# A Strassen down-projection for four more blocks of the middle group, and fewer modulation steps in an opening head

## The chip, the core and the metric

The kernel runs on one core of a Trainium2 chip. The core has five engines, each with its own instruction stream: TensorE (PE, with its weight loads in a row of its own, PEld), VectorE (DVE), ScalarE (ACT), GpSimd (POOL) and SyncE (SP), whose queue issues nearly all transfers of this kernel, in order. The metric is device time in microseconds: of the kernel before, the median of 3 runs is 2173.13 (2171.32 to 2175.94).

## What is computed

One layer of a hybrid streaming encoder over 2112 tokens (2048 of a prompt and 64 of a second sequence) of width 1024, in float32:

```python
mod = (c_act @ w_ada + b_ada)[:, None, :]
sh1, sc1, gt1, sh2, sc2, gt2 = jnp.split(mod, 6, -1)
h = rmsnorm(x, g1) * (1 + sc1) + sh1
proj = h @ w_in
...
hs, C, n, m = mlstm_seq(q, k * HEAD_DIM ** -0.5, v, ig, lf, C, n, m)
...
x = x + gt1 * (jnp.concatenate([pool_out, hs], -1) @ w_out)
h2 = rmsnorm(x, g2) * (1 + sc2) + sh2
up = h2 @ w_up
upp = jnp.concatenate([conv_buf, up], 1)
conv = b_conv + sum(w_conv[j] * upp[:, j:j + T] for j in range(3))
a, g = jnp.split(conv, 2, -1)
x = x + gt2 * ((silu(g) * a) @ w_down)
y = rmsnorm(x, g_final)
```

`w_up` is 1024 x 5632 (two halves, a and g, of 2816 = 22 blocks of 128) and `w_down` 2816 x 1024. The modulation has 6 parts of 1024, from `w_ada`.

## The kernel before

**Precision.** Each float32 operand of a large matrix product is split into a rounded high part and the rest, and three matmuls (the list PASSES) make one product. For a weight unit of 128x512, ScalarE copies the high part (line 411) and VectorE subtracts it from the whole (line 414). Units come in a fixed order, the list `stream`, through the SP queue, some loads ahead.

**Attention part**, about the first 800 us: four groups of 512 tokens (the last of 576). Each has a v projection, four heads, the pooling mixer and an output projection. For a head, `proj_qko` makes q, k and the output gate by `gemm` (line 478), and `lstm` the recurrence; there kw (made on VectorE, helper line 250) feeds the matmuls of line 1323. Beside them run generators that give one step at a tick: lists `bg[0]` to `bg[4]`. `bg[3]` is the modulation: `ada` makes one part of it in 16 steps, each with a load of 128x512 of `w_ada` (line 194, tile raw), three steps ahead, and two VectorE operations (lines 208 and 210). `bg[4]` is `up_sums`, which makes sums of quarters of `w_up` for Strassen's scheme: two loads (line 857), four VectorE adds of 128x256 (876 to 881), one store to `wsum` (867). `gemm` ticks `bg[3]` once inside its loop and once at its end:

```python
        for i in (1,) if calm else (1, 3):
            tick(i)
```

`calm` is a list which is filled ahead of group 0's first head and emptied behind that head's `proj_qko`. In groups 1 to 3 it stays empty. The order of instructions on each engine is fixed when the kernel is built; in the attention groups by a scheduler, in the FFN as written.

**FFN part**, from about 800 us: three groups of 704 tokens. In every group a class `Pair` handles one block f of a and g: its up-projection is Strassen's scheme, seven products of 12 matmuls of 352 columns (line 1594), whose partial results are combined by ScalarE and VectorE (lines 1603, 1607, 1641, 1724); then the convolution's three taps (the first on ScalarE, line 1567, two on VectorE, line 1572), silu (1781), the gate's product (1786, 1789) and the split of the result (`split_hi`, `split_lo`, 1864, 1869). All are put between the next pair's products.

Several blocks at a time are projected down and added to x. `PARTS` says which: group 0 has parts of 5, 5, 6, 6 blocks, groups 1 and 2 parts of 4, 4, 4, 4, 6. Parts of four blocks in groups 1 and 2 (`paired`) go by Strassen's scheme too: the quad is held until the next pair's products have been issued, and `quad_down` then makes it, 168 matmuls of 352 columns (line 2037) with 14 weight units (from `w_quad` and from `dsum`, sums that `quad_sums` makes in group 0), 24 additions to x (`rows_add`, line 2009), and copies of partial sums from one bank to another. One product of the current pair (`last_product`) and its combinations go between them. In place of a copy, ones times a tile can open a bank (`seed`, `take(True)`). The other parts go by `down` (line 2160): per row block n (8) and block k, three matmuls for each of two sections of 448 and 256 columns; block 20's gate and block 21's taps stand in `todo` and are taken one by one between them.

**Between two FFN groups.** `prepare` (in `bg[1]`) normalizes the next group's input and stores seven combinations of it (B11, T1, T2, B21, B22, T3, T4) in DRAM; `reload` loads them (line 692) in the last part of the group. In that last part, `fsq_acc` squares each finished row of x on ScalarE (line 2000) and adds it up on POOL (line 2001), and in the next group's first products `final` (in `bg[0]`) makes the last norm (lines 1901, 725, 726, 1910) and stores y (line 1914).

Of the kernel before, what the change touches and what calls it, by code (L numbers as in the profile page):

```python
# [9 lines left out]
F32 = mybir.dt.float32  # L10
F32R = mybir.dt.float32r
AF = mybir.ActivationFunctionType
ALU = mybir.AluOpType
# [18 lines left out]
ENDS = ((0, 448), (448, 704))  # L32
PARTS = (((0, 5), (5, 10), (10, 16), (16, 22)),) + (((0, 4), (4, 8), (8, 12), (12, 16), (16, 22)),) * 2
NQ = 4

# [29 lines left out]
def tile_layer(ctx: ExitStack, tc: tile.TileContext, xT, vecs, cst, rst, w_mod, w_ada, w_qkou, w_v, w_pool,  # L65
# [264 lines left out]

    dsum = dr.tile([8, P, 4, 512], F32, tag="dsum", name="dsum")

# [9 lines left out]
    for g in range(NFG):  # L342
        held = None
        late = []
        for (f0, f1_) in PARTS[g]:
            for f in range(f0, f1_):
                stream += [(up_unit(f, 0), 512), sum_unit(g, f, WS1)] + late
                stream += [sum_unit(g, f, WS2), (up_unit(f, 1), 512)] + [sum_unit(g, f, i) for i in (WS4, WS3)]
                late = [(up_unit(f, 3), 512)]
                if held is not None:  # L350
                    stream += quad_units(held, late)
                    held, late = None, []
            if paired(g, (f0, f1_)):
                held = f0 // NQ
                continue
            order = down_order(f1_ - f0)
            ends = g == NFG - 1 and f1_ == NF
            seen = set()
            for i, (n, k) in enumerate(order):
                if i == f1_ - f0 - 2:  # L360
                    stream += late
                c = f0 + k // 4 * 4
                if k % 4 == 0 or (n, c) not in seen:
                    seen.add((n, c))
                    d = min(c + 4, f1_)
                    stream.append((w_down[n, :, c * P:d * P], (d - c) * P, OUT, None, ends and n >= NE))
            late = []
# [477 lines left out]
    if True:  # L845
# [604 lines left out]
        for o in groups:  # L1450
# [28 lines left out]
            q1 = None  # L1479
            if o.g == 0:  # L1480
                calm.append(1)
            for hd in range(NH):
# [62 lines left out]
    def both_of(a, b):  # L1545
        return lambda: (a(), b())
# [34 lines left out]
    def behind():  # L1581

        while later:
            later.pop(0)()
# [33 lines left out]

    free = []

    def take(seeded=False):

        while len(free) + len(used) < 6:
            free.append(Bank())
        i = next((i for i, bk in enumerate(free) if bk.wide >= FH), 0) if seeded else 0
        bk = free.pop(i)
        used.append(bk)
        if seeded and bk.wide < FH:
            pe.matmul(bk.t[:, :FH], ones_r, B[-1].at("B11", 0, 0), start=True, stop=True)
            bk.start(FH)  # L1630
        return bk
# [11 lines left out]
    def quad_sums():  # L1643

        for d in range(8):
            for c in (0, 256):
                t = f2.tile([P, 2, FT], F32R, tag="av", name="qs", bufs=AVB)
                w = t.bitcast(F32).rearrange("p a t -> p (a t)")[:, :1024].rearrange("p (i c) -> p i c", i=4)
                nc.sync.dma_start(out=w, in_=w_quad[d, :, :, c:c + 256])
                for _ in range(5):  # L1650
                    yield
                a11, a12, a21, a22 = (w[:, i] for i in range(4))
                dve.tensor_tensor(out=a22, in0=a21, in1=a22, op=ALU.add)
                yield
# [32 lines left out]
    class Pair:  # L1687


        ended = False  # L1690
        quad = None

# [75 lines left out]
        def taps_a(self):  # L1768
            for j in (1, 0):
                conv_tap(self.o, self.f, self.ea, self.ta, j)  # L1770

        def last_product(self):
# [88 lines left out]
        def split_hi(self):  # L1861
            self.d = f2.tile([P, 2, FT], F32R, tag="av", name="av", bufs=AVB)
# [8 lines left out]

    def reload(Bo):
        for nm in BN:
            Bo.load(nm)
            yield
            yield
# [17 lines left out]

    def final(o, x3, ssum):
        for _ in range(4):
            yield
# [11 lines left out]
        for k in range(KD):  # L1909
            dve.scalar_tensor_tensor(out=x3[k], in0=x3[k], scalar=V[:, V_GF + k:V_GF + k + 1], in1=box[0],  # L1910
                                     op0=ALU.mult, op1=ALU.mult)
            yield
            yield
            nc.sync.dma_start(out=yT[k, :, o.t0:o.t0 + FT], in_=x3[k])
            yield
            yield

# [76 lines left out]

    def fsq_acc(ssum, src, lo, hi, first):
        if first:
            act.activation(ssum[:, lo:hi], src, AF.Square)
        else:
            s = fscr()
            act.activation(s[:, lo:hi], src, AF.Square)  # L2000
            pool.tensor_tensor(out=ssum[:, lo:hi], in0=ssum[:, lo:hi], in1=s[:, lo:hi], op=ALU.add)

# [8 lines left out]

    def quad_down(o, quad, cur, done):

# [6 lines left out]
        def duo(d):  # L2020
            units, banks = {}, {}

            def half_product(nm, role, X, op, first=False):
# [18 lines left out]
                if X == 1:  # L2042
                    live[0] -= 1
                behind()

# [32 lines left out]
            if d == 0:  # L2078
                cur.sum_g0()
                cur.shut = True  # L2080
            copy("2B", "1B")
            if d == 0:
# [28 lines left out]
    for o in fgroups:  # L2111
        Bo = B[o.g]
        held = None
        for pi, part in enumerate(PARTS[o.g]):
# [8 lines left out]
            for f in range(f0, f1_):  # L2123
                old, pair = pair, Pair(o, Bo, f, f - f0, av, quad)
                pair.products(old)
                if o.g == 0 and len(x3) < KD or pi == 0 and not bg[0]:
                    x3 += load_x2(o, range(len(x3), min(len(x3) + 2, KD)))
                if held is not None:
                    quad_down(o, held, pair, old)
                    held = None  # L2130
# [3 lines left out]
            if not o.last:  # L2134
# [4 lines left out]
                if lastp:  # L2139
                    drain(0, 1)  # L2140
                    B.append(Sums())
                    bg[1].append(reload(B[-1]))
            if lastp:
# [50 lines left out]

            old = pair.before
            todo.extend([both_of(pair.sum_g1, old.gate), both_of(pair.sum_a, old.split_hi), both_of(old.split_lo, pair.scale_a)])
            for n in range(NE - 1):
                bks.append([take() for _ in ENDS])
                down(bks[n], Ws[n], range(nf - 2), ENDS, plain=n == 0)
                if n == 0:  # L2200
                    do(9)
# [21 lines left out]
        if not o.last:  # L2223
            drain(1)
            bg[0].append(final(o, x3, ssum))
            x3 = []
# [87 lines left out]
```

## Time and profile before

| | |
|---|---|
| median of 3 runs | 2173.13 us |
| profiled execution | 2174.68 us |
| its span | 2172.9 us |
| granted TensorE clock | 0.998 |
| DMA, mean | 248 GB/s |
| attention part, FFN groups 0, 1, 2 begin near | 0, 800, 1258, 1710 us |

The profile is one execution. A row of a timeline has a start, a length, the engine, the line, the operation, what it writes and reads, its shape and, in brackets, how long the engine stood idle ahead of it and what ended that. A row with xN stands for N instructions. Lines that begin with a line number and an engine are groups: count, busy time, mean length in ns, idle time ahead of them.

### The profile page before, as it was taken

The numbers are of one execution on the slowest core, as the hardware profiler recorded it, in microseconds if no ns is written. First come the engines' busy times: TensorE is split into PE (matmuls) and PEld (weight loads), VectorE is DVE, ScalarE is ACT, GpSimd is POOL, SyncE is SP. The second block draws the span as 40 slices with busy tenths as digits, with TensorE's granted clock in tenths as the row PEclk, the third lists the DMA queues.
The fourth block names the chain that finished last, engine by engine and source line by source line (L and its number), as shares of the span: only waits on it lengthen the run. The fifth ranks groups of instructions, "written<-read, shape, count | busy, mean of one in ns | idle before, by whom it ended". The sixth has DMA issues, their size and how long they took to land.

```text
span 2172.9 us, 38060 instructions
## 1 busy us (share of the span) xinstructions
PE 2151.4 (99%) x13553; PEld 2044.4 (94%) x13553; DVE 1634.9 (75%) x3040; ACT 1096.1 (50%) x2181; POOL 258.4 (12%) x475
## 2 busy tenths in 40 slices
PE   8999999999999999999999999999999999999998
PEld 7888888888899999999999999999999999999998
DVE  5878668667955778797967668888886597887874
ACT  4554335334333446464736445655655365565554
POOL 0010000001000201010101220100101321111112
PEclk9999999999999999999999999999999999999999
DMA  8987997987888477888967976666668675555542
GB/s 319 328 305 233 323 321 246 309 302 244 301 283 288 169 260 239 282 292 300 350 214 255 321 245 222 234 208 209 228 222 274 223 255 186 170 177 190 171 160 77
DMA packets 297351, 539.51 MB, mean 248 GB/s; under 512 B 25760, under 2 KB 114336, under 8 KB 297160
## 3 DMA queue, kind: packets, MB, share of 16 engines
q1 hardware_dynamic: 286568, 511.87, 69.6%
q10 hardware_dynamic: 10592, 25.20, 3.0%
q8 instruction: 107, 1.75, 0.3%
q14 instruction: 84, 0.69, 0.1%
HBM read 410.98 MB, written 125.98 MB: 247 GB/s over the span
## 4 chain that ended last, share of the span: by engine, by line
PE 85%; DMA 5%; DVE 5%; issue 2%; ACT 2%; SPq 0%; POOL 0%; DVEq 0%; ACTq 0%; POOLq 0%
PE mm L1594 34%; PE mm L478 22%; PE mm L2160 12%; PE mm L2037 8%; PE mm L1133 3%; DVE wt L414 1%; DMA wt<-wsum 1%; PE m L1323 1%; DMA hl_kept<-wt 1%; PE m L1308 1%; PE m L1343 1%; PE m L1345 1%; DVE tg L1572 1%; DMA raw<-w_qkou 0%; ACT wt L411 0%
## 5 line engine op out<-in xcount | busy, mean ns | idle before, releaser
L1594 PE MATMUL mm<-hx,wt 128*128 128x352 f32 x5544 | 885.9, 321 | 0.7 <-DVE wt L414 0.5
L1594 PEld LDWEIGHTS mm<-hx,wt 128*128 128x128 f32 x5544 | 878.7, 188 | 2.6 <-DVE wt L414 2.0
L478 PE MATMUL mm<-hl,wt 128*128 128x512 f32 (+2 forms) x1920 | 387.4, 357 | 0.0
L411 ACT ACTIVATE wt<-raw 128x512 fp32r<-128x512 f32 (+3 forms) x470 | 276.6, 597 | 177.6 <-PE mm L478 52.8
L478 PEld LDWEIGHTS mm<-hl,wt 128*128 128x128 f32 x1920 | 316.4, 189 | 47.7 <-issue 4.4
L414 DVE TENSOR_TENSOR wt<-raw,wt 128x512 fp32r<-128x512 f32 (+3 forms) x470 | 312.8, 672 | 61.9 <-ACT wt L411 61.7
L2160 PE MATMUL mm<-av,wt 128*128 128x448 f32 (+1 forms) x1632 | 262.7, 322 | 0.0
L2160 PEld LDWEIGHTS mm<-av,wt 128*128 128x128 f32 x1632 | 250.4, 188 | 11.1
L2009 DVE SCALAR_TENSOR_TENSOR x<-mm,MOD,x 128x352 f32<-128x352 f32 (+3 forms) x360 | 167.5, 505 | 77.7 <-PE mm L2160 64.3
L2037 PE MATMUL mm<-av,wt 128*128 128x352 f32 x1344 | 220.7, 323 | 1.9 <-DVE x L2009 0.7
L2037 PEld LDWEIGHTS mm<-av,wt 128*128 128x128 f32 x1344 | 215.4, 188 | 5.0 <-DVE ea L1603 3.0
L1641 ACT ACTIVATE mm<-mm 128x352 f32<-128x352 f32 x196 | 87.8, 448 | 233.7 <-PE mm L1594 177.1
L478 PE MATMUL mm<-mx,wt 128*128 128x512 f32 (+1 forms) x960 | 182.9, 352 | 0.3 <-DVE scr L250 0.3
L478 PEld LDWEIGHTS mm<-mx,wt 128*128 128x128 f32 x960 | 159.4, 188 | 23.0 <-PE mm L478 0.5
L1572 DVE SCALAR_TENSOR_TENSOR ta<-ea,V,ta 128x704 f32<-128x704 f32 (+1 forms) x132 | 125.7, 953 | 58.4 <-ACT ta L1567 54.4
L1572 DVE SCALAR_TENSOR_TENSOR tg<-eg,V,tg 128x704 f32<-128x704 f32 (+1 forms) x132 | 125.7, 952 | 56.8 <-ACT tg L1567 54.3
L414 DVE TENSOR_TENSOR wt<-wt 128x512 fp32r<-128x512 f32 x196 | 133.0, 685 | 12.8 <-ACT wt L411 12.7
L411 ACT ACTIVATE wt<-wt 128x512 fp32r<-128x512 f32 x196 | 119.2, 622 | 36.6 <-DMA wt<-wsum 35.7
L1550 POOL COPY ea<-UC 128x2 f32<-128x2 f32 x66 | 33.1, 501 | 506.2 <-DVE ta L1572 407.3
L1781 ACT ACTIVATE tg<-tg 128x704 f32<-128x704 f32 (+1 forms) x66 | 52.5, 795 | 71.8 <-DVE tg L1572 71.8
L1133 PE MATMUL mm<-wt,hl 128*128 128x256 f32 (+1 forms) x576 | 71.4, 284 | 0.0
L1133 PEld LDWEIGHTS mm<-wt,hl 128*128 128x128 f32 x576 | 70.4, 190 | 0.8 <-issue 0.6
(305 smaller groups left out, 2207.0 us busy)
## 6 DMA issues: line engine op xcount, KB each, us to landing
wt<-wsplit SPq DMA_DIRECT2D x132, 512.0 KB, 4.3
raw<-w_up SPq DMA_DIRECT2D x198, 256.0 KB, 3.8
wt<-hl_kept SPq DMA_DIRECT2D x96, 512.0 KB, 6.3
wt<-wsum SPq DMA_DIRECT2D x132, 256.0 KB, 5.0
wsplit<-wt SPq DMA_DIRECT2D x66, 512.0 KB, 5.1
w<-w_up SPq DMA_DIRECT2D x88, 256.0 KB, 4.4
wsum<-w SPq DMA_DIRECT2D x44, 512.0 KB, 5.9
Bd<-fscr ACTq DMA_DIRECT2D x56, 352.0 KB, 4.3
```

Source lines behind the costliest of these rows:

```text
L411: act.activation(u.w[:, 0, :u.n], u.raw[:, :u.n], AF.Copy)
L414: dve.tensor_tensor(out=u.w[:, 1, :u.n], in0=u.raw[:, :u.n], in1=u.w[:, 0, :u.n].bitcast(F32), op=ALU.subtract)
L478: pe.matmul(ps[bi][:, :hi - lo], U[:, a, k % 4 * P:(k % 4 + 1) * P], mv[k][:, b, lo:hi], start=(at == 0 and pi == 0), stop=(k == order[-1] ...
L1133: pe.matmul(ps[ti][:n, :cols], h[4 * kh + k4][:, b, lo:lo + n], U[:, a, k4 % 2 * cols:(k4 % 2 + 1) * cols], start=(kh == 0 and k4 == 0 and ...
L1550: pool.tensor_copy(ext[:, 0:2], UC[:, f, :])
L1572: dve.scalar_tensor_tensor(out=t[:, :E], in0=ext[:, j:j + E], scalar=wc(j, f), in1=t[:, :E], op0=ALU.mult, op1=ALU.add)
L1594: pe.matmul(bk.t[:, :FH], U[:, a, kc * P:(kc + 1) * P], Bo.at(nm, kc, b), start=(first and kc == 0 and pi == 0), stop=(kc == 3 and pi == 2 ...
L1641: act.activation(to.t[:, :FH], bk.t[:, :FH], AF.Copy)
L1781: act.activation(self.tg[:, :E], self.tg[:, :E], AF.Silu)
L2009: dve.scalar_tensor_tensor(out=x3[n][:, a:b], in0=bk.t[:, a - lo:b - lo], scalar=gt2(n, s), in1=x3[n][:, a:b], op0=ALU.mult, op1=ALU.add)
L2037: pe.matmul(bk.t[:, :FH], U[:, a, c:c + P], quad.put(op, m, b), start=(first and m == 0 and pi == 0), stop=(m == 1 and pi == 2), skip_grou ...
L2160: pe.matmul(bks[i].t[:, :hi - lo], U[:, a, k % 4 * P:(k % 4 + 1) * P], av[k][:, b, lo:hi], start=(k == 0 and (a, b) == PASSES[0]), stop=(k ...
```

## The change

1. **Parts.** In the middle group (group 1) the last part of six blocks becomes a quad of blocks 16 to 19 and a plain part of blocks 20 and 21. `quad_sums` makes ten double sums in place of eight (16 more VectorE adds, 4 more loads and 4 more stores of 512 KB, in group 0).
2. **That quad** is held until the products of block 21 have been issued, and `quad_down` gets `last=True`: behind every second half product it takes one piece from `todo`: block 21's scale, its four taps one by one, silu, gate, split. Blocks 20 and 21 keep their results in tiles of the next group's inputs, so the last of these (T4) is loaded after the part; the other six are loaded in another order. A seed reads a tile of the quad (list `seeds`).
3. **Squares.** Group 1's rows are squared at the opening of the next group, in `final`, eight on ScalarE, with seven additions on VectorE in place of POOL's; its steps stand one or two ticks otherwise.
4. **Modulation.** `calm` is filled ahead of the first head of every attention group.

In the order of instructions, TensorE has 24 matmuls less (288 of line 2160 become 96 of it and 168 of line 2037), POOL 7 additions less, SP 14 quad units and 8 of 128x256 where there were 16 plain ones. In the attention part TensorE's order differs only in a few small matmuls of a modulation part that come one head later in group 3; VectorE's and SP's differ in groups 1 and 2.

```diff
-PARTS = (((0, 5), (5, 10), (10, 16), (16, 22)),) + (((0, 4), (4, 8), (8, 12), (12, 16), (16, 22)),) * 2
-NQ = 4
+PARTS = (((0, 5), (5, 10), (10, 16), (16, 22)), ((0, 4), (4, 8), (8, 12), (12, 16), (16, 20), (20, 22)),
+         ((0, 4), (4, 8), (8, 12), (12, 16), (16, 22)))
+NQ, QUADS = 4, 5
...
-                if held is not None:
+                if held is not None and (f1_ - f0 > 2 or f == f1_ - 1):
                     stream += quad_units(held, late)
...
-            if o.g == 0:
-                calm.append(1)
+            calm.append(1)
...
-            pe.matmul(bk.t[:, :FH], ones_r, B[-1].at("B11", 0, 0), start=True, stop=True)
+            pe.matmul(bk.t[:, :FH], ones_r, seeds[-1](), start=True, stop=True)
...
-        for d in range(8):
+        for d in range(2 * QUADS):
...
-    def reload(Bo):
-        for nm in BN:
+    def reload(Bo, names):
+        for nm in names:
...
-    def final(o, x3, ssum):
-        for _ in range(4):
+    def final(o, x3, ssum, squares):
+        for n in range(KD if squares else 0):
+            fsq_acc(ssum, x3[n], 0, FT, n == 0, dve)
+            yield
+        for _ in range(8 if squares else 4):
             yield
...
                 if X == 1:
                     live[0] -= 1
+                    if last:
+                        do()
...
+                if last:
+                    todo.extend([both_of(cur.scale_a, cur.scale_g)] + [cur.tap(*c) for c in ("a1", "a0", "g1", "g0")]
+                                + [cur.silu, cur.gate, cur.split_hi, cur.split_lo])
...
-                if held is not None:
+                if held is not None and nf > 2:
                     quad_down(o, held, pair, old)
...
+                    if nf == 2:
+                        for p in (old, pair):
+                            p.d = f1.tile([P, 2, HX], F32R, tag="hx", name="av", bufs=2 * len(BN))
                     B.append(Sums())
-                    bg[1].append(reload(B[-1]))
+                    bg[1].append(reload(B[-1], ("B11", "T1", "T2", "B21", "B22", "T3") if nf == 2 else BN))
+            if held is not None and nf == 2:
+                q = held
+                seeds.append(lambda: q.put("B11", 0, 0))
+                quad_down(o, q, pair, old, True)
+                behind()
+                do(9)
+                seeds.pop()
+                held = None
...
-                if not lastp:
+                if not lastp or nf == 2:
                     return
...
-            bg[0].append(final(o, x3, ssum))
+            if nf == 2:
+                Bn = B[-1]
+                Bn.load(BN[-1])
+            bg[0].append(final(o, x3, ssum, nf == 2))
```

More of the change, by code (lines that the diff above doesn't have):

```diff
@@ L329, in sum_unit @@
         return (kept, 512, WHOLE, None) if g else (wsum[f, :, i], 512, INSIDE, kept)
-    dsum = dr.tile([8, P, 4, 512], F32, tag="dsum", name="dsum")
+    dsum = dr.tile([2 * QUADS, P, 4, 512], F32, tag="dsum", name="dsum")
     def quad_units(p, first):
@@ L1619, in tile_layer @@
     free = []
+    seeds = [lambda: B[-1].at("B11", 0, 0)]
     def take(seeded=False):
@@ L1690, in tile_layer @@
         ended = False
-        quad = None
+        quad = d = None
         def __init__(self, o, Bo, f, i, av, quad=None):
@@ L1770, in taps_a, with tap, step @@
                 conv_tap(self.o, self.f, self.ea, self.ta, j)
+        def tap(self, what, j):
+            def step():
+                if what == "a":
+                    conv_tap(self.o, self.f, self.ea, self.ta, int(j))
+                else:
+                    conv_tap(self.o, NF + self.f, self.eg, self.tg, int(j))
+            return step
         def last_product(self):
@@ L1861, in split_hi @@
         def split_hi(self):
-            self.d = f2.tile([P, 2, FT], F32R, tag="av", name="av", bufs=AVB)
+            self.d = self.d or f2.tile([P, 2, FT], F32R, tag="av", name="av", bufs=AVB)
             for (a, b, s) in self.o.segs:
@@ L1915, in final @@
             yield
-            yield
+            if not squares:
+                yield
     late, YLATE = [], 6
@@ L1993, in final_end, with fsq_acc @@
         yield
-    def fsq_acc(ssum, src, lo, hi, first):
+    def fsq_acc(ssum, src, lo, hi, first, adds=pool):
         if first:
@@ L2000, in fsq_acc @@
             act.activation(s[:, lo:hi], src, AF.Square)
-            pool.tensor_tensor(out=ssum[:, lo:hi], in0=ssum[:, lo:hi], in1=s[:, lo:hi], op=ALU.add)
+            adds.tensor_tensor(out=ssum[:, lo:hi], in0=ssum[:, lo:hi], in1=s[:, lo:hi], op=ALU.add)
     ET = mybir.EngineType
@@ L2010, in rows_add, with quad_down @@
                                          in1=x3[n][:, a:b], op0=ALU.mult, op1=ALU.add)
-    def quad_down(o, quad, cur, done):
+    def quad_down(o, quad, cur, done, last=False):
         count = []
@@ L2193, in tile_layer @@
             bks = []
-            old = pair.before
-            todo.extend([both_of(pair.sum_g1, old.gate), both_of(pair.sum_a, old.split_hi), both_of(old.split_lo, pair.scale_a)])
+            if nf > 2:
+                old = pair.before
+                todo.extend([both_of(pair.sum_g1, old.gate), both_of(pair.sum_a, old.split_hi),
+                             both_of(old.split_lo, pair.scale_a)])
             for n in range(NE - 1):
@@ L2199, in tile_layer @@
                 down(bks[n], Ws[n], range(nf - 2), ENDS, plain=n == 0)
-                if n == 0:
+                if n == 0 and nf > 2:
                     do(9)
@@ L2266 @@
     w_down = blocks(i["w_down"][0], NF)
-    six = w_down.reshape(2, 2, 2, P, NF, P)[:, :, :, :, :4 * NQ].reshape(2, 2, 2, P, 4, 2, 2, P)
-    w_quad = six.transpose(4, 1, 3, 0, 6, 2, 5, 7).reshape(8, P, 4, 512)
+    six = w_down.reshape(2, 2, 2, P, NF, P)[:, :, :, :, :QUADS * NQ].reshape(2, 2, 2, P, QUADS, 2, 2, P)
+    w_quad = six.transpose(4, 1, 3, 0, 6, 2, 5, 7).reshape(2 * QUADS, P, 4, 512)
     arrays = {
```

## The prediction

> **What bounds the kernel now.** I read the busy table first, then TensorE's waits, its timeline around the edits, and only then the other engines in those stretches.
>
> ```profile
> span 2172.9 us, 38060 instructions
> PE 2151.4 (99%) x13553; PEld 2044.4 (94%) x13553; DVE 1634.9 (75%) x3040; ACT 1096.1 (50%) x2181; POOL 258.4 (12%) x475
> ```
>
> TensorE (PE) works 2151.4 of 2172.9 us: all its holes together are 21.5 us. So only two things move the time: matmuls taken out, and holes made or closed. The list of TensorE's waits names the holes that matter here:
>
> ```profile
> PE m L1323 <- DVE kw L250: 1.9, 1, 1.9
> PE mm L2037 <- DVE x L2009: 0.7, 1, 0.7
> PE mm L2037 <- DVE wt L414: 0.4, 1, 0.4
> PE mm L2037 <- DVE ea L1603: 0.3, 1, 0.3
> ```
>
> The first is in an attention group's opening head, the other three in Strassen down-projections (line 2037). The profiled execution took 2174.68 us, 1.78 around its span, and lies 1.55 above the median of 2173.13; the sum below is made against 2174.68 and carried over to the median as a difference.
>
> **Term 1, the matmuls.** The middle group's last part had 6 plain blocks, 8 rows x 6 blocks x 3 passes x 2 sections = 288 matmuls. It becomes 2 plain blocks (96) and a Strassen quad of 168 half-width ones; products and seeds stay. TensorE's timeline gives the pitch of each kind (sections of 448 and 256 average 352 columns):
>
> ```profile
> 1331.03 23.21 PE L2037 MATMUL mm<-av,wt 128*128 128x352 f32 x144
> 1354.08 51.47 PE L1594 MATMUL mm<-hx,wt 128*128 128x352 f32 x324
> ...
> 1667.95 42.15 PE L2160 MATMUL mm<-av,wt 128*128 128x448 f32 x264
> 1709.94 4.91 PE L1594 MATMUL mm<-hx,wt 128*128 128x352 f32 x30
> ```
>
> Plain: (1709.94 - 1667.95) / 264 = 0.1591 us. Quad: (1354.08 - 1331.03) / 144 = 0.1601. Out go 192 x 0.1591 = 30.5, in come 168 x 0.1601 = 26.9: **-3.6 us**, if TensorE stays full.
>
> **Term 2, does VectorE (DVE) keep up in the new quad?** By stretches (columns: length, PE, PEld, DVE, ACT, POOL busy, clock, DMA share, GB/s), the second half of group 0's FFN, two neighbouring quads, and the part that is replaced with what follows it:
>
> ```profile
> 1150.00:1195.00 45.00, 45.00 (x286) 45.00 (x285) 35.82 (x51) 30.35 (x54) 7.36 (x13) 1.00 0.76 247
> ...
> 1486.00:1516.00 30.00, 28.98 (x180) 28.40 (x179) 28.00 (x52) 16.49 (x33) 1.31 (x2) 1.00 0.57 187
> 1567.00:1598.00 31.00, 30.58 (x188) 29.76 (x188) 29.06 (x55) 16.36 (x33) 1.31 (x2) 1.00 0.59 187
> ...
> 1662.00:1710.00 48.00, 48.00 (x304) 46.06 (x303) 28.00 (x41) 16.94 (x29) 11.13 (x8) 1.00 0.82 267
> ...
> 1738.00:1777.00 39.00, 39.00 (x248) 39.00 (x247) 34.22 (x58) 24.35 (x44) 11.67 (x24) 1.00 0.79 289
> ```
>
> The replaced part leaves VectorE 20 us idle of 48. A quad fills it. What the new one holds, from the groups of VectorE in the two neighbouring quads:
>
> ```profile
> L2009 DVE SCALAR_TENSOR_TENSOR x<-mm,MOD,x 128x352 f32<-128x352 f32 x48 | 26.3, 580 | 3.4 <-PE mm L2037 3.2
> L414 DVE TENSOR_TENSOR wt<-wt 128x512 fp32r<-128x512 f32 x19 | 13.0, 685 | 0.0
> L1572 DVE SCALAR_TENSOR_TENSOR ta<-ea,V,ta 128x704 f32<-128x704 f32 x8 | 7.6, 952 | 5.4 <-ACT ta L1567 5.2
> L1813 DVE TENSOR_TENSOR av<-tg,av 128x704 fp32r<-128x704 f32 x6 | 5.3, 888 | 0.1
> L1603 DVE TENSOR_TENSOR ea<-mm,s 128x352 f32<-128x352 f32 x5 | 2.6, 517 | 0.0
> ```
>
> 24 row adds x 0.580, 16 weight splits (14 quad units at 0.685, two of 128x256 at 0.42, as the add of that size at 437.80 below), 4 taps x 0.952, 4 gate and split operations of 704 at about 0.888 and 3 small ones x 0.517: 13.9 + 10.4 + 3.8 + 3.6 + 1.6 = 33.3. Neighbours overlap by about 0.09 (below, an operation of 0.69 at 437.20 is followed at 437.80), so 50 of them take 33.3 - 50 x 0.085 = 29.1. TensorE has 168 + 12 matmuls there, 180 x 0.160 = 28.8. The two are level, as in the neighbours, which stall 0.7 + 0.3 in one and 0.4 in the other. Taking block 21's taps singly is what keeps one wait from being a whole block's chain. I take the mean of those two, **+0.7**; ends 0 and +2 (all four taps, 3.8, half hidden).
>
> **Term 3, the squares that move.** Behind a row's add, the old last part squares it on ScalarE and adds on POOL. While that add runs, VectorE's operation beside it stretches:
>
> ```profile
> 1694.43 1.70 POOL L2001 TENSOR_TENSOR ssum<-ssum,fscr 128x704 f32<-128x704 f32 x1 [4.02 <-ACT fscr L2000]
> ...
> 1694.85 1.84 DVE L414 TENSOR_TENSOR wt<-raw,wt 128x512 fp32r<-128x512 f32 x1 [1.05 <-ACT wt L411]
> ```
>
> 1.84 against 0.685. Seven of them would have cost a full VectorE up to 7 x 1.15 = 8 us; they go, so nothing of it falls on the quad. [...] In their place 8 squares on ScalarE and 7 adds of 0.888, 6.2 us of VectorE, stand in the next group's first products. The next 39 us stretch (1738) has VectorE at 34.22, but 1710 to 1738 is emptier, and the weight splits run some products ahead: **+0.3**, ends 0 and +1.5.
>
> **Terms at nothing.** Two more double sums in group 0 add 16 operations of 128x256, 16 x 0.33 = 5.3 us of VectorE and 8 x 0.5 MB; VectorE has 9.2 us free in the 45 us from 1150, and 4.2 MB over 45 us lift 247 to 340 GB/s. Cover gone, 5.3; I keep 0 to +0.5. The quad's units are 1.6 MB more than the old part's, over 46 us: 267 to 302 GB/s, below the 289 to 340 that run with TensorE full: 0, end +1. That the last of the next group's sums (T4) is loaded after the part is within this.
>
> **Term 4, the modulation steps.** An item on the list makes each matrix product's end tick one list instead of two, so half of a group's 16 modulation steps (two VectorE operations and one weight load of 256 KB each) leave the opening head and fall into the next. Since the orders of VectorE and of the SP queue are fixed in advance, this reorders both. Before, around group 2's opening head:
>
> ```profile
> 427.40 0.75 DVE L210 SCALAR_TENSOR_TENSOR s<-raw,CA,s 128x512 f32<-128x512 f32 x1 [4.35 <-DMA raw<-w_ada]
> ...
> 433.46 0.75 DVE L210 SCALAR_TENSOR_TENSOR s<-raw,CA,s 128x512 f32<-128x512 f32 x1 [4.49 <-DMA raw<-w_ada]
> ...
> 437.20 0.69 DVE L250 TENSOR_TENSOR kw<-m,CL 128x512 f32<-128x512 f32 x1
> 437.80 0.42 DVE L881 TENSOR_TENSOR w<-w 128x256 f32<-128x256 f32 x1
> ```
>
> ```profile
> 438.03 1.65 PE L1323 MATMUL m<-va,kw 128*128 128x129 f32 x8 [1.85 <-DVE kw L250]
> ```
>
> ```profile
> 421.76 0.56 SPq L867 DMA_DIRECT2D wsum<-w  x1
> 422.37 0.62 SPq L194 DMA_DIRECT2D raw<-w_ada  x1
> ...
> 425.46 2.02 SPq L857 DMA_DIRECT2D w<-w_up  x2
> 427.53 1.11 SPq L194 DMA_DIRECT2D raw<-w_ada  x2
> ```
>
> ```profile
> raw<-w_ada SPq DMA_DIRECT2D x48, 256.0 KB, 5.4
> ```
>
> Here VectorE twice sits over 4 us on a modulation weight, and that makes kw late by 1.85. In the new order fewer steps stand ahead of kw, but the last one's load stands on SP directly behind a store of up-projection sums (line 867), and that store waits for VectorE to end two interleaved sets of sums; the second set's own weights wait for the store issued at 421.76. By the rows: weights issued near 425.5, landed 5 later at 430.5 (5.0 is 422.37 to 427.40), two sets of four adds x 0.33 (0.42 less the overlap) end near 433, store and load issued 433.1 and 433.7, landed 5.4 later at 439.1, one step 0.66, kw 0.69: 440.4, where it ended 437.89. That is +2.5; with a landing of 4.4 it is +1.5, which I take since fewer of these loads are then under way; ends -1.85 (the hole closes) and +4. In group 2's second head one load again stands behind such a store: +0.5, ends 0 and +2. Group 1's opening head has no hole; its second head has three steps ahead of kw, two of them behind a store that waits for VectorE. The step that runs at 272.38 now has lost 2 us of such work ahead of it, so I put the store at 270:
>
> ```profile
> 272.38 0.74 DVE L210 SCALAR_TENSOR_TENSOR s<-raw,CA,s 128x512 f32<-128x512 f32 x1
> ...
> 279.12 1.05 PE L1323 MATMUL m<-va,kw 128*128 128x129 f32 x8
> ```
>
> Issued 270.9 and 271.5, landed 276.9, four operations x 0.66 and kw 0.69: about 279.6 against the 279.12 that TensorE keeps now, +0.6, ends 0 and +2.6. Group 3's order ahead of kw is unchanged: 0. Together **+2.6**.
>
> [...]
>
> **Sum.** -3.6 + 0.7 + 0.3 + 2.6 = 0.0: 2174.7 where the profiled run was, **2173** for the median.
>
> **Rivals.**
> A. The steps put off really free VectorE: group 2's hole of 1.85 closes and no other opens. For it: 8.8 us of VectorE waits sit directly ahead of kw, and fewer steps are left there; if the loads land in 3 to 4 us, all three stalls of term 4 are gone. Against it: the store that now stands before the load. -3.6 - 1.85 + 0.7 = -4.8, **2168.4**.
> B. The other side: the modulation loads stick behind the sums' stores in both groups. Each of the three places takes its upper end less a third, 2.7 + 1.3 + 1.7 = 5.7, and as a late head puts off the next store too, up to 8.6. With term 1 to 3 (-2.6): +3.1 to +6.0, **2178** in the middle. It decides once term 4 passes 7. For it: every step of that chain is in the rows; against: landings are as often short as long.
> C. The change gives only its matmuls: attention shifts but no wait changes, -2.6, **2170.5**.
> D. The change does not do what it says, since the quad is bound by VectorE: term 2 at +2 and term 3 at +1.5 eat the 3.6, with term 4 in the middle +2.5, **2175.6**.
>
> **How the numbers follow.** 0.2%, 4.35 us, is about what a measurement of this kernel can tell from no change. Forecast 0.30, A 0.33, B 0.23, C 0.08, D 0.06. A is as likely as the forecast by itself, but C and D are the forecast with one term at its end, so the middle holds 0.44 and gives the time. A's -4.8 lies little beyond the bound, and I count three quarters of it, 0.25, with 0.06 from the lower ends of the forecast and C: faster 0.31. Slower: three quarters of B, 0.17, and 0.07 from the upper ends of the forecast and D: 0.24. Same: 0.45. The likeliest alone, 2170 to 2176; with A and B the range goes down to 2167 and up to 2180.
>
> **What would show it.** Term 1: 264 matmuls where 288 stood, the next group's first product 3 us sooner after the part's start. Term 2: waits at line 2037 on x, wt or a tap. Term 3: a wait of line 1594 on a weight split in group 2's first four products. Term 4: the wait of line 1323 on kw, in each attention group, and the SP row of the load ahead of it. The forecast is wrong if kw's wait vanishes (A) or passes 7 us in sum (B), or if TensorE waits elsewhere for more than 2 us.

## The result and the profile after

The changed kernel takes 2190.45 us (median of 5 runs, 2188.68 to 2194.78) against 2173.13: a ratio of 1.0080, with a 95% interval from 1.0064 to 1.0095. It is 17 us slower where no change was forecast, and outside the range. The profiled execution has a span of 2187.9 us, 15.0 more than before.

TensorE's busy line and its list of waits in the changed kernel (line numbers of the attention part are one higher than before):

```profile
PE 2152.9 (98%) x13529; PEld 2044.6 (93%) x13529; DVE 1663.4 (76%) x3107; ACT 1103.5 (50%) x2201; POOL 246.4 (11%) x468
...
PE m L1324 <- DVE kw L251: 8.7, 3, 4.0
...
PE m L1378 <- DVE kw L251: 3.2, 1, 3.2
PE mm L1594 <- DVE wt L415: 1.9, 2, 1.1
PE mm L2051 <- DVE x L2023: 1.4, 2, 0.7
```

The 24 matmuls are gone (13553 to 13529), yet TensorE is busy 1.5 us longer. That is a sign to look at its clock, and it will be needed below. Waits on kw have grown from 1.9 to 11.9 us.

To see where the 15.0 us are, I set the start of the same work in both traces side by side:

| work that starts | before | after | later by |
|---|---|---|---|
| group 1, first head (line 1230, 1231 after) | 248.10 | 248.82 | 0.7 |
| group 2, first head | 426.12 | 430.58 | 4.5 |
| group 3, first head | 618.15 | 626.26 | 8.1 |
| first product of the FFN | 791.78 | 806.08 | 14.3 |
| first quad of FFN group 1 | 1324.95 | 1340.03 | 15.1 |
| middle group's replaced part | 1662.18 | 1677.40 | 15.2 |
| first product after it | 1709.94 | 1723.27 | 13.3 |
| first quad of FFN group 2 | 1776.60 | 1791.61 | 15.0 |

So attention group 1 costs 3.7 us, group 2 3.7 and group 3 with what follows it 6.2. The replaced part gains 1.9, and the next group's opening gives back 1.7. The rest I take for scatter of loads, as the 0.7 in group 0, where the order of instructions is the same. Part 4 of the change, the line about `calm`, is nearly the whole loss; the Strassen part is nearly nothing.

**The holes.** TensorE's timeline of the changed kernel at the three places in groups 1 and 2, and at one in group 3:

```profile
283.48 1.16 PE L1324 MATMUL m<-va,kw 128*128 128x129 f32 x8 [3.46 <-DVE kw L251]
...
444.60 1.13 PE L1324 MATMUL m<-va,kw 128*128 128x129 f32 x8 [3.96 <-DVE kw L251]
...
468.82 1.16 PE L1324 MATMUL m<-va,kw 128*128 128x129 f32 x8 [1.29 <-DVE kw L251]
...
694.43 0.98 PE L1378 MATMUL m<-V,nd 128*128 128x128 f32 x5 [3.23 <-DVE kw L251]
```

VectorE's timeline before three of them. In each, an operation on a late load stands just ahead of kw, and VectorE, in order, waits with it:

```profile
280.09 0.75 DVE L211 SCALAR_TENSOR_TENSOR s<-raw,CA,s 128x512 f32<-128x512 f32 x1 [4.63 <-DMA raw<-w_ada]
...
440.96 0.75 DVE L211 SCALAR_TENSOR_TENSOR s<-raw,CA,s 128x512 f32<-128x512 f32 x1 [3.09 <-DMA raw<-w_ada]
...
443.11 0.75 DVE L211 SCALAR_TENSOR_TENSOR s<-raw,CA,s 128x512 f32<-128x512 f32 x1 [0.65 <-DMA raw<-w_ada]
443.78 0.68 DVE L251 TENSOR_TENSOR kw<-m,CL 128x512 f32<-128x512 f32 x1
...
692.46 0.58 DVE L738 SCALAR_TENSOR_TENSOR mx<-mx,G,mx 128x352 f32<-128x352 f32 x1 [9.58 <-DMA mx<-x2d]
```

And SP's own queue of the changed kernel shows when each load went out, and behind what:

```profile
274.23 0.56 SPq L868 DMA_DIRECT2D wsum<-w  x1
274.84 1.90 SPq L195 DMA_DIRECT2D raw<-w_ada  x2
...
433.16 0.59 SPq L195 DMA_DIRECT2D raw<-w_ada  x1
436.24 0.56 SPq L868 DMA_DIRECT2D wsum<-w  x1
436.84 0.83 SPq L195 DMA_DIRECT2D raw<-w_ada  x1
...
680.09 0.57 SPq L868 DMA_DIRECT2D wsum<-w  x1
...
684.17 1.20 SPq L858 DMA_DIRECT2D w<-w_up  x2
...
686.08 0.59 SPq L751 DMA_DIRECT2D mx<-x2d  x1
```

In groups 1 and 2 a modulation load follows the store of the sums, which waits for VectorE (3.8 us ahead of 274.23, 2.7 ahead of 436.24): issued at 274.84 and landed at 280.09, issued at 436.84 and landed at 443.11. In group 2's opening head that is the smaller part, 0.65 us of waiting. The longer wait there, 3.09, is for the load ahead of the store: it was issued at 433.16 and took 7.7 us to land, where the median of these loads is 5.1. In group 3 it is another load. The two loads of `w_up` reuse a buffer, so they wait for the store of 680.09 to land, until 684.17; the row of x for the FFN's first norm (mx) is behind them and lands at 692.46. Before, SP had the row ahead of these two loads:

```profile
675.91 0.56 SPq L867 DMA_DIRECT2D wsum<-w  x1
...
677.21 0.97 SPq L750 DMA_DIRECT2D mx<-x2d  x1
679.48 1.20 SPq L857 DMA_DIRECT2D w<-w_up  x2
```

**The Strassen part.** TensorE's timeline of the replaced part and of the opening behind it:

```profile
1677.40 4.34 PE L2051 MATMUL mm<-av,wt 128*128 128x352 f32 x24
...
1693.26 14.69 PE L2051 MATMUL mm<-av,wt 128*128 128x352 f32 x90 [0.73 <-DVE x L2023]
1707.78 15.65 PE L2190 MATMUL mm<-av,wt 128*128 128x448 f32 x96
...
1778.51 13.26 PE L1594 MATMUL mm<-hx,wt 128*128 128x352 f32 x82 [1.11 <-DVE wt L415]
```

The quad has one wait on a row's add, and the opening a wait on a weight split, which VectorE makes late behind the last norm.

**The clock.** The hole that ends at 694.43 cost more than its 3.23 us. By stretches of the changed kernel (columns as in the prediction; the clock is the third from the right) after it:

```profile
694.40:697.00 2.60, 2.39 (x13) 1.73 (x17) 2.57 (x8) 1.37 (x3) 0.00 (x0) 0.60 1.01 357
697.00:700.00 3.00, 3.00 (x13) 1.34 (x10) 2.04 (x4) 0.68 (x1) 0.33 (x2) 0.50 0.83 288
700.00:703.00 3.00, 3.00 (x18) 2.76 (x17) 1.03 (x4) 0.00 (x0) 0.00 (x0) 0.71 0.71 235
```

The granted clock falls to 0.50 and is 1.00 again from 703 to 706. As an estimate from these rows, at 0.60, 0.50 and 0.71 the three stretches lose 2.6 x 0.40 + 3.0 x 0.50 + 3.0 x 0.29 = 3.4 us. In them TensorE counts as busy and gets on more slowly: the matmuls of 256 columns of line 479 are 0.26 us apart from 698.72 and 0.14 from 703.08. The same was there before, after the one hole of 1.85 us:

```profile
438.00:441.00 3.00, 2.97 (x12) 2.72 (x13) 2.90 (x9) 0.00 (x0) 0.00 (x0) 0.58 1.05 407
441.00:445.00 4.00, 4.00 (x24) 3.51 (x24) 2.76 (x8) 0.37 (x2) 0.00 (x0) 0.89 0.43 156
```

By the same estimate 3.0 x 0.42 + 4.0 x 0.11 = 1.7 us, so that hole cost 3.5. After the 3.46 us at 283 the clock stayed at 1.00 (283.5 to 287.5).

The attention part adds up: holes of 3.46 + 3.96 + 1.29 + 3.23, 1.26 at the output projection and 0.18 elsewhere, 13.4 against 3.0 before, make 10.4 more; low clock, by the estimate, 1.7 (0.74 from 444.6 to 447, 0.64 from 447 to 450) + 3.4 against 1.7, 3.4 more: 13.8, where the table has 3.7 + 3.7 + 6.2 = 13.6.

### The profile page after: what moved, and what is told of

Read it like the earlier page. It is cut to its first block, busy times and chain, and to the rows that moved or that the text cites. A ratio compares the mean times of both kernels' runs of the same rounds, so it can differ in the third digit from the quotient of the medians.

```text
span 2187.9 us, 38117 instructions
## 1 busy us (share of the span) xinstructions
PE 2152.9 (98%) x13529; PEld 2044.6 (93%) x13529; DVE 1663.4 (76%) x3107; ACT 1103.5 (50%) x2201; POOL 246.4 (11%) x468
## 4 chain that ended last, share of the span: by engine, by line
PE 80%; DVE 7%; DMA 7%; issue 2%; ACT 2%; SPq 1%; POOL 0%; DVEq 0%; ACTq 0%; POOLq 0%
PE mm L1594 35%; PE mm L479 18%; PE mm L2190 10%; PE mm L2051 9%; PE mm L1134 2%; DMA raw<-w_ada 2%; DVE wt L415 1%; DMA wsum<-w 1%; DVE tg L1572 1%; PE m L1324 1%; DMA yT<-x 1%; PE m L1344 1%; PE m L1346 1%; DMA mx<-x2d 0%; DVE scr L251 0%
## 5 line engine op out<-in xcount | busy, mean ns | idle before, releaser
L415 DVE TENSOR_TENSOR wt<-raw,wt 128x512 fp32r<-128x512 f32 (+3 forms) x468 | 307.0, 662 | 57.0 <-ACT wt L412 56.3
L2051 PE MATMUL mm<-av,wt 128*128 128x352 f32 x1512 | 248.7, 324 | 2.9 <-DVE x L2023 1.4
L2023 DVE SCALAR_TENSOR_TENSOR x<-mm,MOD,x 128x352 f32<-128x352 f32 (+5 forms) x384 | 180.6, 507 | 68.6 <-PE mm L2190 53.8
L2190 PE MATMUL mm<-av,wt 128*128 128x448 f32 (+1 forms) x1440 | 232.1, 322 | 0.0
L415 DVE TENSOR_TENSOR wt<-wt 128x512 fp32r<-128x512 f32 x204 | 138.3, 683 | 13.5 <-ACT wt L412 13.2
L412 ACT ACTIVATE wt<-wt 128x512 fp32r<-128x512 f32 x204 | 123.7, 622 | 39.1 <-DMA wt<-wsum 36.0
```

The source lines that it names most:

```text
L412: act.activation(u.w[:, 0, :u.n], u.raw[:, :u.n], AF.Copy)
L415: dve.tensor_tensor(out=u.w[:, 1, :u.n], in0=u.raw[:, :u.n], in1=u.w[:, 0, :u.n].bitcast(F32), op=ALU.subtract)
L2023: dve.scalar_tensor_tensor(out=x3[n][:, a:b], in0=bk.t[:, a - lo:b - lo], scalar=gt2(n, s), in1=x3[n][:, a:b], op0=ALU.mult, op1=ALU.add)
L2051: pe.matmul(bk.t[:, :FH], U[:, a, c:c + P], quad.put(op, m, b), start=(first and m == 0 and pi == 0), stop=(m == 1 and pi == 2), skip_grou ...
L2190: pe.matmul(bks[i].t[:, :hi - lo], U[:, a, k % 4 * P:(k % 4 + 1) * P], av[k][:, b, lo:hi], start=(k == 0 and (a, b) == PASSES[0]), stop=(k ...
```

## The experiments

Times are medians, ratios against the kernel before on the same chip, whose medians lay between 2174.0 and 2175.5 in these sessions. T is the theory just told.

**e1, part 4 undone.**

```diff
-            calm.append(1)
+            if o.g == 0:
+                calm.append(1)
```

> Part 4 undone: the list is filled in group 0 alone, the rest of the change stays; the orders of all engines up to the FFN are then those of before. Theory T (the loss of 17 us is made in the attention groups 1 to 3, where loads stand on SP behind entries that wait; the Strassen part gains 1.9 us in its stretch and gives 1.7 back in the next opening): 2172 to 2174 us, and no wait of the recurrence's matmuls on kw over the 1.9 us that the kernel before has. Rival R1 (the FFN edits cost much of it, through 2 more double sums in group 0 and the quad): 2178 or more.

Measured: 2174.34, ratio 1.0003 (0.9994 to 1.0011). R1 falls, and T holds for the time, but not for the wait: on kw it is 2.61 near 438, over the 1.9 that was forecast, though the order there is that of before. With that order the same hole is 1.86 in e3, 2.26 in e7 and 2.33 in e8, so it moves by some 0.8 us from one execution to the next. Parts 1 to 3 together neither gain nor lose.

**e2, part 4 alone on the kernel before.**

```diff
-            if o.g == 0:
-                calm.append(1)
+            calm.append(1)
```

> The kernel before with part 4 alone, so the attention groups run in the order of the changed kernel. T: 2186 to 2190 us, start of the FFN some 13 to 14 us later than before, with waits on kw of some 3.5 us in group 1, 4.0 and 1.3 in group 2 and 3 in group 3. R1: under 2180.

Measured: 2191.33, ratio 1.0082 (1.0069 to 1.0095): all of the loss, 1.3 us above T's range. The FFN begins at 808.43, 16.7 later than before. The waits on kw are 3.68, 4.26, 1.32 and 3.92 us.

**e3, the list filled in groups 0 and 3 only.**

```diff
-            if o.g == 0:
+            if o.g in (0, 3):
                 calm.append(1)
```

> The kernel before with the list filled in groups 0 and 3 only. T: the losses of the groups are made one by one (+3.7 in group 1, +3.7 in group 2, +6.2 in group 3 by the trace), so 2179 to 2180 us, with the wait on kw in group 3's third head. Rival R2 (group 3 only suffers since groups 1 and 2 hand it work late): 2173 to 2175.

Measured: 2183.15, ratio 1.0046 (1.0034 to 1.0058). R2 falls: group 3 makes its loss by itself, and more of it than in the changed kernel and than T allowed, 9 us. Its hole is longer:

```profile
689.33 0.90 PE L1377 MATMUL m<-V,nd 128*128 128x128 f32 x3 [6.08 <-DVE kw L250]
```

The granted clock is 0.55 from 688 to 692 and 0.59 from 692 to 696.

**e4, the loads on another queue.**

```diff
                 got[i] = raw_tile()[:, :512]
-                nc.sync.dma_start(out=got[i], in_=src[i])
+                nc.gpsimd.dma_start(out=got[i], in_=src[i])
...
-            nc.sync.dma_start(out=xs[i], in_=x2d[k, :, t0:t0 + FH])
+            nc.gpsimd.dma_start(out=xs[i], in_=x2d[k, :, t0:t0 + FH])
```

> The changed kernel as a whole, but the modulation weights of groups 1 to 3 (a) and the input rows of the FFN's first norm (b) are loaded from POOL's queue instead of SP's, so that no such load stands behind SP's waiting stores and loads of the up-projection sums. T: VectorE's waits of 4 to 10 us on raw and mx ahead of kw go, and with them most of the 14 us: 2174 to 2179 us. Rival R3 (what makes kw late is VectorE's bunched work or the memory's load, not the place on SP): 2186 or more, with the same waits.

Measured: 2187.15, ratio 1.0057 (1.0045 to 1.0069). This misses: the waits of TensorE on kw are gone from groups 1 to 3, as T has it, but the time falls by only 5 of the 17 us and lies where R3 put it. With a free queue the scheduler has put the modulation steps earlier, into the v projection, and there VectorE waits for them, with a small copy behind it that ScalarE and then TensorE need:

```profile
232.66 3.57 PE L1134 MATMUL mm<-wt,hl 128*128 128x256 f32 x15 [5.41 <-ACT va L251]
```

The edit moved the order of VectorE as well as the place in the queue, so it tells the two apart badly. What it does show is that a step placed ahead of its load's landing made a hole, of 5.41 us, with the load on POOL's queue too.

**e5, group 3's row load one tick sooner, on e3.**

```diff
             nc.sync.dma_start(out=h2d[k, :, t0:t0 + FH], in_=xs[i])
-            yield
             if i > 1 and i + 6 < len(todo):
                 load(i + 6)
+            yield
```

> The kernel of e3 (list filled in groups 0 and 3), but the generator of the FFN's first norm issues its next row load ahead of its yield, one tick sooner. In SP's order the row load (line 751 of this kernel) then stands ahead of the two loads of up-projection weights that wait for a store to land; in e3 it stands behind them. T (place on SP, not the steps themselves): VectorE's wait of 9.6 us on mx and TensorE's hole of 6.1 us at line 1377 go, 2174 to 2177 us. Rival R4 (the steps put off load VectorE or the memory in the third head): 2181 or more.

Measured: 2181.24, ratio 1.0026 (1.0015 to 1.0037). The time alone is at R4's bound, but the loss against the kernel before is 5.8 us where e3 has 9.1. The trace says why it is only part of it: one row load now goes out ahead of the loads of `w_up`, but the next row that VectorE needs ahead of kw is still behind them.

```profile
674.67 0.97 SPq L750 DMA_DIRECT2D mx<-x2d  x1
676.96 1.21 SPq L857 DMA_DIRECT2D w<-w_up  x2
...
679.52 0.42 SPq L750 DMA_DIRECT2D mx<-x2d  x1
```

VectorE waits for it until 684.88, 5.1 us, and TensorE's hole is 3.32 instead of 6.08. So the hole shrinks by nearly half as the load's place changes, with the same steps in the same head.

**e6, both shifts on the changed kernel.** The one of e5, and the store of the sums one step later:

```diff
                 yield
-                store()
                 pin(dve.tensor_tensor(out=a0, in0=g1, in1=a0, op=ALU.subtract))
                 pin(dve.tensor_tensor(out=a1_, in0=a1_, in1=a0, op=ALU.subtract))
-                made.append((f, c, w))
                 yield
+                store()
+                made.append((f, c, w))
```

> The changed kernel as a whole with two shifts: the row load of e5 one tick sooner, and the store of the up-projection sums one step later in its generator. In the order, the modulation loads ahead of kw in group 1's second head and in group 2's opening head then no longer stand behind a store that waits, but ahead of kw in group 2's opening head a set of sums stands whose weights are loaded behind such a store. T: the holes in group 1 (3.5) and group 3 (3.2 and what follows) go, the one in group 2's opening head stays, with w from w_up as VectorE's late load: 2179 to 2183 us. R4: 2188 or more.

Measured: 2176.86, ratio 1.0005 (0.9997 to 1.0014), lower than expected: some 16 of the 17 us return with part 4 in place. In TensorE's timeline the holes of group 1's and group 2's second heads and of group 3's third head are gone, and the one that was to stay stayed. Group 1's second head is the clean case. Two modulation steps of two operations each stand ahead of kw as in the changed kernel, but their loads go out ahead of the store that waits:

```profile
269.58 1.08 SPq L195 DMA_DIRECT2D raw<-w_ada  x2
274.67 0.56 SPq L868 DMA_DIRECT2D wsum<-w  x1
```

```profile
275.92 0.75 DVE L211 SCALAR_TENSOR_TENSOR s<-raw,CA,s 128x512 f32<-128x512 f32 x1 [0.68 <-DMA raw<-w_ada]
...
278.57 0.69 DVE L251 TENSOR_TENSOR kw<-m,CL 128x512 f32<-128x512 f32 x1
```

In group 2's opening head no modulation step is left between the head's start and kw, and on VectorE the late load is now the sums' weights, as forecast:

```profile
439.84 1.85 PE L1324 MATMUL m<-va,kw 128*128 128x129 f32 x8 [2.82 <-DVE kw L251]
```

```profile
438.21 0.42 DVE L877 TENSOR_TENSOR w<-w 128x256 f32<-128x256 f32 x1 [5.41 <-DMA w<-w_up]
```

R4 falls: the steps put off do no harm by themselves that can be told from the scatter. What took the time 2 us below T's range was not shown.

**e7 and e8, the squares.** Both on e1, with the squares back in the part; e8 adds on VectorE instead of POOL.

```diff
-                if not lastp or nf == 2:
+                if not lastp:
...
-            bg[0].append(final(o, x3, ssum, nf == 2))
+            bg[0].append(final(o, x3, ssum, False))
```

and for e8 as well

```diff
-                    fsq_acc(ssum, x3[n][:, lo:hi], lo, hi, n == 0)
+                    fsq_acc(ssum, x3[n][:, lo:hi], lo, hi, n == 0, dve if nf == 2 else pool)
```

> The changed kernel with part 4 undone (as e1) and part 3 undone too: the last norm's squares and POOL's additions stand in the plain part of two blocks again. T3 (the opening of group 2 gives back 1.7 us since squares and additions push the last norm into the later products): the wait of 1.1 us on a weight split near 1763 goes, while VectorE's splits beside POOL's additions stretch to 1.8 us; as the plain part is only 15 us long, some of it shows there: 2172 to 2174 us. Rival R5 (the opening's loss has another cause, the loads): the wait stays, 2174 or more.

> As e7, but the additions in the plain part on VectorE. T3: no stretched splits, the opening as in e7: 2171.5 to 2173.5 us, the lowest of the four without part 4. R5: as e1, 2174 or more.

Measured: e7 2173.78, ratio 0.9990 (0.9981 to 0.9998), e8 2182.73, ratio 1.0034 (1.0022 to 1.0046). e7 agrees with T3: the wait near 1763 (1.13 in e1) is gone, and the opening, from the first product to the first quad, takes 66.95 us where e1 has 68.22, the changed kernel 68.34 and the kernel before 66.66. So the move of the squares made most of what the opening gave back. The stretch expected in the part was not there: few splits fall beside POOL's additions, and the longest lasts 0.80. POOL's seven additions take 13.44 us without a pause, 1.70 to 2.04 each, as in the kernel before. e8 is a miss of 10 us. TensorE and VectorE there:

```profile
1708.75 4.23 PE L1595 MATMUL mm<-hx,wt 128*128 128x352 f32 x24 [1.12 <-issue]
1715.93 2.13 PE L1595 MATMUL mm<-hx,wt 128*128 128x352 f32 x6 [2.95 <-ACT mm L1643]
```

```profile
1709.96 0.89 DVE L2016 TENSOR_TENSOR ssum<-ssum,fscr 128x704 f32<-128x704 f32 x1 [0.92 <-ACT fscr L2015]
1710.77 1.07 DVE L2024 SCALAR_TENSOR_TENSOR x<-mm,MOD,x 128x448 f32<-128x448 f32 x2
1712.76 0.89 DVE L2016 TENSOR_TENSOR ssum<-ssum,fscr 128x704 f32<-128x704 f32 x1 [0.92 <-ACT fscr L2015]
```

A row's add (VectorE), its square (ScalarE) and its addition (VectorE) form a ring between two engines: 2.8 us a row (1709.96 to 1712.76), where TensorE makes a row in 15.5 / 8 = 1.9. The rows run late, the first copies of the next group (line 1643) stand behind the squares, and after the hole the clock is 0.50 from 1716 to 1724. In e7, with the additions on POOL, VectorE's row adds of 1704 to 1711 us wait for TensorE alone, 0.73 us at most, and a row takes 1.93 (1706.72 to 1708.65).

**e9, the sums held in group 2's opening head, on the kernel before.**

```diff
+    hush = []
...
-            if at in ups and not quiet:
+            if at in ups and not quiet and not hush:
                 tick(4)
...
+            if o.g == 2:
+                hush.append(1)
             for hd in range(NH):
                 qko = proj_qko(o, h, q1)
...
                 calm.clear()
+                hush.clear()
```

> The kernel before, with one edit: during group 2's opening head the generator of the up-projection sums isn't ticked (a list, hush, like the list calm). Ahead of kw there, the modulation loads then stand on SP behind no store that waits. Theory T+G (a late load makes the hole, and after the hole TensorE's granted clock is low for some us, so a hole of 1.9 us costs about 3.5): the hole at line 1323 near 438 goes, the granted clock from 436 to 444 stays at 1.00, 3 to 4 us less than before, ratio 0.9985. Rival R6 (the clock dips there for another reason): at most 1.9 us less, the dip stays.

Measured: 2177.07, ratio 1.0012 (1.0002 to 1.0021), where 0.9985 was forecast. Locally as forecast: no hole, the granted clock at 1.00 from 432 to 444, and the FFN begins at 788.82, 3.0 sooner than before. R6 falls. But TensorE stalls as the FFN begins:

```profile
792.00:796.00 4.00, 1.64 (x8) 0.88 (x6) 4.00 (x10) 1.95 (x5) 0.00 (x0) 1.00 0.67 205
796.00:800.00 4.00, 1.41 (x5) 1.41 (x6) 3.55 (x9) 2.45 (x5) 0.00 (x0) 0.62 0.19 74
800.00:804.00 4.00, 4.00 (x16) 4.00 (x15) 1.09 (x2) 0.98 (x2) 0.00 (x0) 0.52 0.81 248
```

VectorE is full there, TensorE has a hole of 4.56 us and the clock falls: the gain is given back. What fills VectorE is not the sums, whose last addition is at 746.41 (740.19 before), but the combinations of the FFN's first input (lines 771 and 775 of this kernel). The last store of the sums lands at 751.4 in place of 743.8, and in both traces ScalarE's queue sends the first loads of that input (fscr from h2d) within 0.4 us of this landing, at 751.48 in place of 744.20. So the held sums put off the loads, and the loads the combinations. That these loads wait for that store is read from the times, not tested.

**e10, that edit with parts 1 and 2.** Its edit is that of e9 on e7.

> The edit of e9 with parts 1 and 2 of the change, without parts 3 and 4 (as e7): the two gains are in different stretches, so they add, 1.7 to 2 us of the Strassen part and 3 to 4 of the hole: 5 to 6 us less than before, ratio 0.9975. If the hold pushes sums into later heads that then stall, 0 to 3 less.

Measured: 2175.06, ratio 0.9999 (0.9990 to 1.0009). By its time this is the second case, but the stall is at another place: no later head has it, the FFN's start again has a hole of 4.0 us.

**e11, the two shifts on the kernel before.** The edits of e5 and e6 without part 4.

> The kernel before with the two shifts of e6 (store one step later, row load one tick sooner), without part 4: a control for e6. T: the kernel before has only the hole in group 2 to mend, and there a late set of sums stays ahead of kw: within 3 us of before. If it is 8 us or more faster, e6's return was not the mending of what part 4 had broken, but a gain of its own.

Measured: 2173.69, ratio 0.9995 (0.9986 to 1.0003). So e6's return of some 16 us is the mending of part 4's damage, no gain of its own. The hole in group 2 is 3.01 here, without a dip of the clock.

**e12, parts 1 and 2 with the shifts.** e7 with the edits of e5 and e6.

> Parts 1 and 2 of the change without parts 3 and 4 (as e7), and the two shifts of e6. e7 gave a ratio of 0.9990, the shifts alone 0.9995 (e11, within its interval of 1): if they add, 0.9985, 3 us less than before, with the one hole in group 2's opening head left and none at the FFN's start. If the shifts do nothing, 0.9990.

Measured: 2171.79, ratio 0.9983 (0.9974 to 0.9992), as forecast if the two add, though the interval doesn't exclude the 0.9990 of the other case. This beats both kernels: 2.9 us below the 2174.70 of before in its session, with the hole in group 2's opening head (1.86, then a clock of 0.57) still in it.

## Why the prediction was wrong

**Term 4 failed**, and it alone accounts for the miss: +2.6 forecast, ends -1.85 and +8.6, measured +13.6. Four steps in it, the first the largest:

- "Group 3's order ahead of kw is unchanged: 0." I had compared the opening head only. The account of the change ahead of the prediction has the same fault where it lets SP's order differ in groups 1 and 2 alone: in group 3 the row load and the two loads of `w_up` have changed places. The steps put off change the third head, where the late load is no modulation weight but a row for the next norm. It cost 6.2 us, and 9 by itself (e3). The search was for modulation loads behind stores; the question should have been for any load behind any entry that waits.
- A hole was priced at its length. Its cost here was the length and what the low clock took after it, by the estimate above 3.4 us after the hole in group 3 and 1.7 after the one in group 2, in the kernel before too.
- Group 1's second head, +0.6 forecast, was 3.7. The chain was right and its start was not: the store was put at 270 and went out at 274.23, since the sums ahead of it had not moved forward by the 2 us that I assumed (the last ended near 274.2, before near 274.5). From there all came more than 3 us later. The sum was off as well: four operations and kw, 4 x 0.66 + 0.69 from 276.9, end at 280.2 and not at 279.6, so these rows gave +1.1.
- Group 2's opening head came near in size, partly by luck. Store and load were put at 433.1 and 433.7; they went out at 436.24 and 436.84 in a group that began 4.5 us later, so 1.3 sooner than forecast, and the landing took 6.3 where I took 4.4. The longer wait was for the load ahead of the store, with its landing of 7.7 us, which the forecast hadn't in it. The hole grew by 2.1 where I took 1.5, against a scatter of some 0.8. The second head has a hole of 1.29 for 0.5.

It is rival B that came nearest, "the modulation loads stick behind the sums' stores", with its point of decision (term 4 over 7) passed by far. Its price went no higher than 8.6, since it lacked group 3's row load and the clock.

**Terms 1 and 2** gave -1.9 for -2.9. The matmuls are 24 fewer as worked out. The quad's 168 took 4.2 + 24.3 us for the 26.9 of their pitch, 1.6 more, twice the 0.7 I chose and inside the ends of 0 and 2. VectorE's part that a wait shows is 0.73, on x at 1693. Another 0.3 lies in the first 24 matmuls, which take 4.2 us in the quads of before too (1324.95 to 1329.13) and weren't in the pitch. The rest is put to no wait.

**Term 3** was mis-sized: +0.3 forecast, 1.7 measured, just over its end of 1.5, and e7 shows the squares as the cause of most of it. What I held against leaving them in the part, 7 x 1.15 us of stretched VectorE, did not come: in e7 the splits there last 0.80 at most, against 0.685.

**Terms at nothing**: the FFN's group 0, with the additional sums, begins 14.3 later and ends 15.1 later. The same stretch, with the same double sums, takes 532.2 us in e1 and 533.0 in e7, against 533.2 before and 534.0 in the changed kernel, so I take it for scatter. The 302 GB/s of the quad's units were called below rates that run with TensorE full, but only the 289 was measured, and the 340 was an estimate of mine; TensorE's one wait in the new quad is not on a load.

## What to carry to other kernels

When an edit moves background work, don't look only at the engine that it relieves: read the in-order load queue for every load that now stands behind an entry that waits, and price it at queue wait and landing together. Where the engines' orders are fixed in advance, as here, a step whose load lands late holds up what stands behind it (VectorE waited 9.58 us for a row ahead of kw in group 3), so the place of the load decided more than the amount of work (e6: all the steps still put off, some 16 us less). And don't price a hole of TensorE by its length alone: with the low clock behind it, as estimated above, the one of 1.85 cost 3.5 here, the one of 3.23 cost 6.6, the one of 3.46 only its length.

## What the runs showed of the hardware

- Ten holes of TensorE, each with the mean of the granted clock in a stretch of 4 us at its end or behind it: 1.85 us in the kernel before, 0.57 (438 to 442); 1.86 in e12, 0.57 (440 to 444); 2.95 in e8, 0.50 (1716 to 1720); 3.01 in e11, 1.00 (439 to 443); 3.23 in the changed kernel, 0.56 (694.4 to 698.4); 3.46 in the changed kernel, 1.00 (283.5 to 287.5); 3.68 in e2, 0.57 (283 to 287); 3.96 in the changed kernel, 0.64 (444.6 to 448.6); 4.56 in e9, 0.52 (800 to 804); 6.08 in e3, 0.55 (688 to 692). So the clock was low after eight of them and not after those of 3.01 and 3.46, the latter in the same order of work as e2's 3.68. As an estimate from these means, 4 x 0.36 = 1.4 to 4 x 0.50 = 2.0 us were lost in the 4 us where it was low. Nothing read here tells which holes have it.
- In the part that is replaced, VectorE's subtraction of 128x512 took 1.84, 1.84 and 1.85 us beside POOL's additions of 704 columns (1.70 us each) in the kernel before (at 1689.13, 1694.85 and 1700.62), 1.07 beside the first two, of 1.98 and 2.04 (1683.70), and 0.69 and 0.68 with POOL idle (1666.51 and 1675.17). In e7, where POOL adds without a pause, the splits took 0.80 at most. So the stretch didn't come with every addition.
